# A two-layer trunk on one core: first stage in a pinned order, second shift in halves of 1024 columns, scaling on ScalarE

## The chip, the cores and the metric

The kernel runs on one core of one Trainium2 chip. The metric is the time of one execution in microseconds (us); the program is one launch. The core has five engines that work side by side, each through its own list of instructions in order: TensorE (PE; its weight loads are shown as PEld), VectorE (DVE), ScalarE (ACT), GpSimd (POOL) and SyncE (SP), which here mainly issues transfers. 16 DMA engines move data between the chip's memory and the core.

## The reference, cut to what matters

256 tokens of 2048 channels (two blocks of 128 tokens) go through two layers; everything is float32.

```python
cond = silu(c)
for l in range(2):
    sh1, sc1, g1, sh2, sc2, g2 = split(cond @ ada_w[l] + ada_b[l], 6)   # ada_w[l]: 2048 x 12288
    h = rmsnorm(x, norm_mix_g[l]) * (1 + sc1) + sh1
    y = mixer_ab(h, ...) if l == 0 else mixer_c(h, ...)
    x = x + g1 * y
    h = rmsnorm(x, norm_ffn_g[l]) * (1 + sc2) + sh2
    x = x + g2 * ((silu(h @ w1) * (h @ w3)) @ w2)                        # w1, w3: 2048 x 5632
return rmsnorm(x, final_g)
```

`mixer_ab` projects h through `w_in` (2048 x 4096) into four parts of 1024 columns, does a gated convolution over 31 tokens on two of them and a gated mixing of tokens inside chunks of 128 on the other two, and projects the result through `w_out`. `mixer_c` is a pooling over windows of tokens with a small projection.

## The kernel before, in words

**Products.** Each product of an activation with a weight is made from three of the chip's faster kind: weight and activation are split into a high part and a rest (`hi`, `lo` for weights, `ah`, `al` for activations), and hi x ah, hi x al and lo x ah are added up in PSUM. A weight block `raw` is 256 rows x 512 columns (512 KB). ScalarE casts it to `hi` (L167), VectorE subtracts (`lo`, L168), TensorE multiplies (L216, L217, L222). A `unit` is 512 rows x 512 columns: two such blocks, 24 products for the two blocks of tokens. There are 12 `raw` buffers and 4 each of `hi` and `lo`.

**Conditioning.** The six vectors of a layer are sums over the 2048 rows of `ada_w`, weighted by `cond`. They come in 512 KB blocks too, by one of two ways. On TensorE (`on_pe`, L381): products with a broadcast `cond` into the PSUM tile `ps_ada`, copied to `rows` (L395). On VectorE: multiply-adds into `accq` (512 columns, `mod_cols`, L388) or `acc` (1024 columns, `weighed` and `mod_full`, L353). Then `put_cols` turns the row into columns by small products (`ps_col`, L408) and VectorE adds the bias (L414, L417). These are Python generators: each `yield` ends a step, and the steps stand in one list, `bg`. After each unit `tick` adds the current rate to a credit and takes that many whole steps (`RATES`: 1.28 a unit in the first mixer, 0.71 in the first feed-forward).

**Entry of a stage.** An `Entry` holds what a normalised input needs. `sumsq` (ScalarE, L459) and `rstd` (VectorE and GpSimd) give the factor r of a block of tokens; `transposed` multiplies by r (VectorE, L477) and transposes 512 channels (TensorE, `tp`, L480); `prep_plain` copies that out (`xT`, ScalarE, L518). `scaled` applies scale and shift, two of four tiles on ScalarE (L500) and two on VectorE (L502), and splits the result (`ah`, ScalarE, L489; `al`, VectorE, L490). So an input can be transposed before its scale and shift are known.

**Stages that begin before their conditions are complete.** `started` takes the rows of three column blocks in four quarters of 512 rows. Ahead of a quarter it scales the input with that quarter's columns; while it multiplies, `between` advances the generators of the next quarter's scale and shift (`e.parts`), one step in each of the slots 0 to 3 and all the rest in slot 4. There are six slots in a quarter, one behind each half unit. The rate is 0 meanwhile. It is used for the first mixer (`w_in`, `params` laid out behind its first quarter) and for the first feed-forward (`w1`, `w3`). The first mixer's scale is summed on TensorE, its shift on VectorE but for the first quarter.

**Order.** The program is written as above; a planner then orders each engine's list, by the program's order as priority and by estimated durations, so that an instruction may be moved ahead of others. Transfers of blocks are issued by SP. The small parameters (`stage`, `st_b`, `prm`, `nrm`) are issued from ScalarE's queue at the start. `x` is loaded first. In the first mixer the list `bg` holds the gate (`gen_g1`, 16 steps on TensorE), the second scale (four quarters of 5 steps, on TensorE) and the second shift (four quarters of 5 steps, on VectorE, `accq`). What is left of the shift at the end is done inside the feed-forward's `started`.

Of the kernel before, what the change touches and what calls it, by code (L numbers as in the profile page):

```python
# [8 lines left out]
F32 = mybir.dt.float32  # L9
F32R = mybir.dt.float32r  # L10
AF = mybir.ActivationFunctionType
ALU = mybir.AluOpType
PSUM = bass.MemoryType.PSUM

P = 128
# [21 lines left out]
class Trunk:  # L37
# [6 lines left out]
    def __init__(self, ctx, tc, ins, out):  # L44
        self.ctx, self.tc, self.nc = ctx, tc, tc.nc
        self.i, self.out = ins, out
        self.bg = []
        self.credit = 0.0
        self.late = []
        self.fill = []  # L50

        def pool(name, bufs, **kw):
# [12 lines left out]
        self.tpp = pool("tpp", 2, space=PSUM)  # L65
        self.adap = pool("adap", 1, space=PSUM)
        self.msp = pool("msp", 1, space=PSUM)


    def consts(self):  # L70
        nc, c = self.nc, self.cpool
        i = self.i
        cs = self.wk.tile([KT, P], F32, name="cs", tag="t", bufs=3)
        nc.sync.dma_start(out=cs, in_=i["c"].rearrange("a (k p) -> (a k) p", p=P))
# [15 lines left out]

        ps = self.msp.tile([P, 512], F32, name="ps_c", tag="ms")
# [3 lines left out]
        stage = self.wk.tile([P, P], F32, name="stage", tag="t", bufs=3)  # L95
        nc.vector.memset(stage, 0.0)
# [10 lines left out]
        put("ffn_g", i["norm_ffn_g"].rearrange("l (k p) -> (l k) p", p=P), 2 * KT)  # L107
        put("conv_b", i["a_conv_b"].rearrange("l (k p) -> (l k) p", p=P), HT)
        put("a_g", i["a_norm_g"].rearrange("l (k p) -> (l k) p", p=P), HT)
        put("a_b", i["a_norm_b"].rearrange("l (k p) -> (l k) p", p=P), HT)  # L110
        put("b_bias", i["b_bias"].rearrange("l h t -> (l h) t"), HT)
        ps = self.msp.tile([P, 512], F32, name="ps_c", tag="ms")
# [5 lines left out]
        self.adab = c.tile([P, 2, 6 * KT], F32, name="adab")  # L118
        for l in range(2):
            st = self.wk.tile([P, P], F32, name="st_b", tag="t", bufs=3)  # L120
            nc.scalar.dma_start(out=st[: 6 * KT, :], in_=i["ada_b"][l].rearrange("(k p) -> k p", p=P))
            ps = self.msp.tile([P, 512], F32, name="ps_b", tag="ms")
            nc.tensor.transpose(ps[:, : 6 * KT], st[: 6 * KT, :], self.ident[: 6 * KT, : 6 * KT])
            nc.vector.tensor_copy(self.adab[:, l, :], ps[:, : 6 * KT])
# [243 lines left out]
    def mod_cols(self, l, v, q, on_pe, dst, gname=None):  # L368
# [7 lines left out]
        for u in range(4):  # L376
# [14 lines left out]
            if u < 3:  # L391
                yield
# [6 lines left out]
        yield  # L399
# [23 lines left out]
    def to_bcast(self, rows, dst, n=4):  # L423

        nc = self.nc
        hi = self.wk.tile([P, 512], F32R, name="rhi", tag="t", bufs=3)
        lo = self.wk.tile([P, 512], F32R, name="rlo", tag="t", bufs=3)
        self.split_act(rows, hi, lo)
        for j in range(n):
            ps = self.msp.tile([P, 512], F32, name="ps_bc", tag="ms")  # L430
            one = self.identr[:, 32 * j : 32 * j + 1].to_broadcast([P, P])
            nc.tensor.matmul(ps, one, hi, start=True, stop=False)
            nc.tensor.matmul(ps, one, lo, start=False, stop=True)
            nc.scalar.copy(dst[:, 512 * j : 512 * j + 512], ps)

    def norm_cols(self, e, l, sc, sh, gname):

        e.parts = [
            self.add(self.mod_cols(l, sc, q, True, e.gs, gname), self.mod_cols(l, sh, q, q == 0, e.sh))
# [33 lines left out]
    def transposed(self, b, q, r):  # L473
# [3 lines left out]
        nc.vector.tensor_scalar(xr, self.x[b][:, 512 * q : 512 * q + 512], r, None, op0=ALU.mult)  # L477
# [14 lines left out]
    def scaled(self, src, q, b, gs, sh):  # L492
# [38 lines left out]
    def between(self, gens, slot):  # L531

        for g in gens:
# [5 lines left out]
    def started(self, e, w_cols, rate, then=None):  # L539
# [8 lines left out]
        for q in range(4):  # L548
            e.act[q] = [self.scaled(e.act[q][b], q, b, e.gs, e.sh) for b in range(NB)]
            nxt = e.parts[q + 1] if q < 3 else ()  # L550
            for u, (w, col0) in enumerate(w_cols):
                self.unit(
                    w, 512 * q, col0, e.act[q], ps[u], q == 0, q == 3, lambda: self.between(nxt, 2 * u)
                )
                self.between(nxt, 2 * u + 1)
            if q == 0 and then is not None:
                then()
# [47 lines left out]
    def mixer_ab(self, e, nxt):  # L605
        nc, i = self.nc, self.i
        with ExitStack() as s:
# [14 lines left out]
            nc.scalar.dma_start(out=ws, in_=i["b_w_s"][0].rearrange("h t s -> t h s"))  # L622
            nc.scalar.dma_start(out=cwr[:CW, :], in_=i["a_conv_w"][0])
            for n, name in enumerate(("b_norm_g", "b_norm_b")):
                nc.scalar.dma_start(out=nrm[0:64:32, n, :], in_=i[name][0].rearrange("(j n) -> j n", n=512))

            def params():

# [4 lines left out]
                for hh in range(2):  # L633
                    ps = self.msp.tile([P, 4, P], F32, name="tp", tag="ms")
                    for a in range(4):
                        nc.tensor.transpose(ps[:, a, :], ws[:, 4 * hh + a, :], self.ident)
                    nc.vector.tensor_copy(wcT[:, 4 * hh : 4 * hh + 4, :], ps)
                    ps = self.msp.tile([P, 4, P], F32, name="tp", tag="ms")
                    for a in range(4):
                        k = 4 * hh + a  # L640
                        nc.tensor.transpose(ps[:, a, :CW], cwr[:CW, k * P : k * P + P], self.ident[:CW, :CW])
                    nc.vector.tensor_copy(cw[:, 4 * hh : 4 * hh + 4, :CW], ps[:, :, :CW])
                self.to_bcast(nrm[:, 0, :], bg, 2)
                self.to_bcast(nrm[:, 1, :], bb, 2)

            for b in range(NB):
                e.start(b)
                for q in range(4):
                    e.prep(b, q)
            held = self.started(e, [(w_in, 0), (w_in, DH), (w_in, 512)], RATES[0], params)  # L650
# [226 lines left out]
    def ffn(self, p, l, e, nxt, gen_g2, rest):  # L877
# [6 lines left out]
        if e.parts:  # L884
# [4 lines left out]
            ps = self.started(e, [(w1, 0), (w3, 0), (w1, 512)], RATES[1])  # L889
            held = {(1, 0): ps[0], (3, 0): ps[1], (1, 1): ps[2]}  # L890
# [76 lines left out]
    def run(self):  # L967
# [3 lines left out]
        self.x = []  # L971
        for b in range(NB):
            xb = self.xpool.tile([P, D], F32, name=f"x{b}")
            nc.sync.dma_start(out=xb, in_=i["x"][0, b * P : (b + 1) * P, :])
            self.x.append(xb)
            for q in range(4):
                self.sumsq(b, q)
# [11 lines left out]
        self.finish(mix0.parts[0][:1])  # L989
# [87 lines left out]
```

## Time and profile before

| | us |
|---|---|
| time, median of 3 runs (2012.48 to 2015.93) | 2014.81 |
| the profiled execution's own time | 2018.89 |
| span of the profiled execution | 2017.2 |
| TensorE busy in it | 1957.5 |
| granted TensorE clock, mean | 0.982 |
| moved by DMA | 540.39 MB, 268 GB/s |

The span is the time from the first to the last instruction. A group's line gives the place in the kernel, the engine, the operation, what it writes and reads, the count, then the busy time and the mean of one in ns, then the idle time of the engine in front of it and who ended it. A line of the timeline begins with its start and its duration in us; in brackets stands the idle time before it and its releaser.

### The profile page before, as it was taken

How to read it: one execution, taken by the hardware profiler on the slowest of the kernel's cores; microseconds unless marked ns; L12 is line 12 of the kernel's file. 1: busy time of each engine (PE TensorE's matmuls, PEld its weight loads, DVE VectorE, ACT ScalarE, POOL GpSimd, SP SyncE). 2: the span in 40 equal slices, each digit the busy share in tenths (PEclk: the TensorE clock that was granted, in tenths of full speed). 3: DMA queues.
4: the chain of work that ended last, by engine and by line, in shares of the span. 5: the costliest groups of instructions: out<-in, count | busy, mean ns of one | idle time of the engine just before them, and what ended most of it. 6: DMA issues, size and time to landing. Idle time of an engine off the chain costs nothing.

```text
span 2017.2 us, 24298 instructions
## 1 busy us (share of the span) xinstructions
PE 1957.5 (97%) x8896; PEld 1542.4 (76%) x8896; DVE 1420.8 (70%) x1709; ACT 840.2 (42%) x1023; POOL 34.2 (2%) x91
## 2 busy tenths in 40 slices
PE   5989999998999999999999999999999999999998
PEld 2567677777887888887878887788788888888886
DVE  2667999788778888777887788867555444554455
ACT  3234343454444334443344347544433444334443
POOL 0000000000000000000120000000000000000000
PEclk9889999989999999999999999999999999999999
DMA  9998988879888899888988887889656666566651
GB/s 329 351 369 266 339 277 284 270 252 343 294 277 327 316 341 331 300 295 316 343 308 292 289 286 264 324 276 326 198 187 191 189 189 191 183 189 190 193 184 48
DMA packets 250344, 540.39 MB, mean 268 GB/s; under 512 B 16521, under 2 KB 17849, under 8 KB 249840
## 3 DMA queue, kind: packets, MB, share of 16 engines
q1 hardware_dynamic: 248472, 536.99, 78.2%
q10 hardware_dynamic: 1752, 1.86, 0.3%
q8 instruction: 69, 1.13, 0.2%
q14 instruction: 51, 0.42, 0.1%
HBM read 536.68 MB, written 2.10 MB: 267 GB/s over the span
## 4 chain that ended last, share of the span: by engine, by line
PE 95%; DVE 2%; DMA 2%; ACT 1%; issue 0%; POOL 0%; ACTq 0%; POOLq 0%; DVEq 0%
PE mm L216 28%; PE mm L217 27%; PE mm L222 27%; PE ps_ada L381 3%; PE ps_col L408 2%; PE mt L216 1%; PE mt L217 1%; PE tp L591 1%; PE mt L222 1%; DVE accq L388 1%; PE ps_ada L315 1%; PE tp L480 1%; DMA st_b<-in_ada_b_dram 1%; PE tp L838 1%; DMA raw<-in_pool_w_dram 0%
## 5 line engine op out<-in xcount | busy, mean ns | idle before, releaser
L167 ACT CAST hi<-raw 128x1024 fp32r<-128x1024 f32 x632 | 665.1, 1053 | 986.1 <-PE mm L217 898.2
L168 DVE TENSOR_TENSOR lo<-raw,hi 128x1024 fp32r<-128x1024 f32 x632 | 771.1, 1223 | 423.6 <-ACT hi L167 413.3
L216 PE MATMUL mm<-hi,ah 128*128 128x512 f32 x1568 | 619.5, 396 | 6.0 <-ACT hi L167 3.4
L217 PE MATMUL mm<-hi,al 128*128 128x512 f32 x1568 | 613.6, 392 | 0.0
L222 PE MATMUL mm<-lo,ah 128*128 128x512 f32 x1568 | 422.9, 390 | 0.0
L216 PEld LDWEIGHTS mm<-hi,ah 128*128 128x128 f32 x1568 | 296.0, 189 | 94.3 <-ACT hi L167 14.4
L217 PEld LDWEIGHTS mm<-hi,al 128*128 128x128 f32 x1568 | 296.1, 189 | 62.9 <-DVE accq L388 1.7
L222 PEld LDWEIGHTS mm<-lo,ah 128*128 128x128 f32 x1568 | 295.6, 189 | 61.7
L216 PE MATMUL mm<-hi,hh 128*128 128x512 f32 x704 | 279.9, 398 | 0.0
L217 PE MATMUL mm<-hi,hl 128*128 128x512 f32 x704 | 277.4, 394 | 0.0
L353 DVE SCALAR_TENSOR_TENSOR acc<-raw,cond,acc 128x1024 f32<-128x1024 f32 x180 | 230.6, 1281 | 5.3 <-DMA raw<-in_ada_w_dram 3.7
L222 PE MATMUL mm<-lo,hh 128*128 128x512 f32 x704 | 194.7, 395 | 0.0
L216 PEld LDWEIGHTS mm<-hi,hh 128*128 128x128 f32 x704 | 132.1, 188 | 34.7 <-ACT hi L167 1.7
L222 PEld LDWEIGHTS mm<-lo,hh 128*128 128x128 f32 x704 | 132.1, 188 | 32.1
L217 PEld LDWEIGHTS mm<-hi,hl 128*128 128x128 f32 x704 | 132.1, 188 | 30.8
L388 DVE SCALAR_TENSOR_TENSOR accq<-raw,cond,accq 128x512 f32<-128x512 f32 x135 | 101.1, 749 | 4.8 <-DMA raw<-in_ada_w_dram 2.1
L676 DVE SCALAR_TENSOR_TENSOR co<-aT,cw,co 128x256 f32<-128x256 f32 x240 | 99.5, 479 | 0.0
L216 PE MATMUL mm<-hi,mh 128*128 128x512 f32 x160 | 64.8, 406 | 1.6 <-ACT mh L489 1.6
L599 DVE TENSOR_TENSOR gy<-mm,gate 128x512 f32<-128x512 f32 x72 | 47.1, 686 | 24.3 <-PE mm L222 23.9
L217 PE MATMUL mm<-hi,ml 128*128 128x512 f32 x160 | 63.8, 401 | 0.3 <-DVE ml L490 0.3
L381 PE MATMUL ps_ada<-raw,cond 128*32 128x512 f32 x352 | 62.3, 629 | 0.0
L600 DVE TENSOR_TENSOR x<-x,gy 128x512 f32<-128x512 f32 x72 | 47.2, 688 | 0.1
(169 smaller groups left out, 990.6 us busy)
## 6 DMA issues: line engine op xcount, KB each, us to landing
raw<-in_ffn_w_dram SPq DMA_DIRECT2D x528, 512.0 KB, 4.8
raw<-in_ada_w_dram SPq DMA_DIRECT2D x384, 512.0 KB, 5.7
raw<-in_ab_w_in_dram SPq DMA_DIRECT2D x64, 512.0 KB, 6.5
raw<-in_ab_w_out_dram SPq DMA_DIRECT2D x32, 512.0 KB, 5.7
raw<-in_pool_w_dram SPq DMA_DIRECT2D x8, 512.0 KB
x<-in_x_dram SPq DMA_DIRECT2D x2, 1024.0 KB, 6.5
gate<-in_final_g_dram SPq DMA_DIRECT2D x1, 1024.0 KB
out_dram<-x SPq DMA_DIRECT2D x2, 512.0 KB
```

Source lines behind the costliest of these rows:

```text
L167: nc.scalar.copy(hi, raw)
L168: nc.vector.tensor_tensor(lo, raw, hi.bitcast(F32), op=ALU.subtract)
L216: nc.tensor.matmul(ps[b], act[b][0][:, kk, :], hi[:, k, :], start=first and kk == 0, stop=False)
L217: nc.tensor.matmul(ps[b], act[b][1][:, kk, :], hi[:, k, :], start=False, stop=False)
L222: self.nc.tensor.matmul(ps[b], act[b][0][:, kk, :], lo[:, k, :], start=False, stop=last and kk == 3)
L353: nc.vector.scalar_tensor_tensor(acc, raw, self.cond[:, k : k + 1], acc, op0=ALU.mult, op1=ALU.add)
L381: nc.tensor.matmul(acc[32 * j : 32 * j + 32, :], self.cond[:, k : k + 1].to_broadcast([P, 32]), raws[j // 2][:, j % 2, :], start=u == 0, s ...
L388: nc.vector.scalar_tensor_tensor(acc, raws[j // 2][:, j % 2, :], self.cond[:, k : k + 1], acc, op0=ALU.mult, op1=ALU.add)
L408: nc.tensor.matmul(ps[:, a : a + 1], src[:, P * a : P * a + P], one, start=u == 0, stop=u == len(parts) - 1,)
L599: nc.vector.tensor_tensor(t, ps, g[:, 512 * q : 512 * q + 512], op=ALU.mult)
L600: nc.vector.tensor_tensor(xs, xs, t, op=ALU.add)
L676: nc.vector.scalar_tensor_tensor(co[:, k, :], src, cw[:, k, j : j + 1], co[:, k, :], op0=ALU.mult, op1=ALU.add,)
```

## The change

It has three parts.

First, the first stage gets a written order. A new method `opening` interleaves the loads of x, the first quarter of scale and shift, and the small parameters, whose transfers move from ScalarE's queue to SP. A new method `staged` replaces `started` for the first mixer: it loads and casts both blocks of a unit ahead of its products, and it puts one step of `params` (now a generator: taps, mixing weights and broadcasts of the tables) behind each half unit from the second quarter on, except in slot 4. The tables' transfers (`tables`) are issued by SP behind the first quarter. `in_order` chains all instructions of TensorE, VectorE, ScalarE and SP that are traced inside it, so that the planner can't reorder them among themselves. In the staged form `mod_cols` leaves out the step between the sum and `put_cols`.

Second, the second shift is summed by `mod_full` in two halves of 1024 columns; `started` also advances the second half during the first quarter (`more`).

Third, a flag `lean` is on from the end of the first stage to the end of the first feed-forward's `started`: the multiplication by r and all four tiles of `scaled` go to ScalarE.

```diff
+    def opening(self, e):
+        nc, c, i = self.nc, self.cpool, self.i
+        sc, sh = e.parts[0]
...
+        def tokens(b):
+            nc.sync.dma_start(out=self.x[b], in_=i["x"][0, b * P : (b + 1) * P, :])
+            for q in range(4):
+                self.sumsq(b, q)
+
+        def entry(b):
+            e.start(b)
+            for q in range(4):
+                e.prep(b, q)
...
         def put(name, ap, n):
-            nc.scalar.dma_start(out=stage[r : r + n, :], in_=ap)
+            nc.sync.dma_start(out=stage[r : r + n, :], in_=ap)
...
+        next(sc)
+        next(sc)
+        tokens(0)
+        next(sc)
         put("mix_g", ...)
+        tokens(1)
+        entry(0)
+        next(sc)
         put("ffn_g", ...)
+        ... loads of ada_b into st_b0, st_b1 ...
+        next(sh)
         put("conv_b", ...); put("a_g", ...); put("a_b", ...); put("b_bias", ...)
+        next(sh)
+        ... transposes of st_b0, st_b1 into adab ...
+        entry(1)
         ... transpose of stage into cols ...
+        self.close(sc)
+        next(sh)
+        next(sh)
+        self.close(sh)
...
-            if u < 3:
+            if u < 3 or staged:
                 yield
...
-        yield
+        if not staged:
+            yield
         self.put_cols(parts, 4, l, v, 4 * q, dst, gname)
...
-        nc.vector.tensor_scalar(xr, self.x[b][:, 512 * q : 512 * q + 512], r, None, op0=ALU.mult)
+        src = self.x[b][:, 512 * q : 512 * q + 512]
+        if self.lean:
+            nc.scalar.activation(xr, src, AF.Copy, scale=r)
+        else:
+            nc.vector.tensor_scalar(xr, src, r, None, op0=ALU.mult)
...
-            if a < 2:
+            if a < 2 or self.lean:
                 nc.scalar.activation(h[:, a, :], src[:, a, :], AF.Identity, scale=g, bias=t)
...
+    def staged(self, e, w_cols, then, extra):
+        self.rate = 0.0
...
+        for q in range(4):
+            e.act[q] = [self.scaled(e.act[q][b], q, b, e.gs, e.sh) for b in range(NB)]
+            nxt = e.parts[q + 1] if q < 3 else ()
+            for u, (w, col0) in enumerate(w_cols):
+                raws = [self.load(w, 512 * q + 256 * h, col0) for h in range(2)]
+                cuts = [self.split(raw) for raw in raws]
+                for h, (hi, lo) in enumerate(cuts):
+                    for b in range(NB):
+                        self.products(hi, lo, h, e.act[q], b, ps[u], q == 0)
+                    for b in range(NB):
+                        self.products_lo(hi, lo, h, e.act[q], b, ps[u], q == 3)
+                    self.between(nxt, 2 * u + h)
+                    if q > 0 and 2 * u + h != 4:
+                        next(extra, None)
+            if q == 0:
+                then()
...
     def started(self, e, w_cols, rate):
...
+            more = e.parts[2][1:] if q == 0 else ()
...
+            with self.in_order():
+                self.opening(e)
+                extra = params()
+                held = self.staged(e, [(w_in, 0), (w_in, DH), (w_in, 512)], tables, extra)
+                for _ in extra:
+                    pass
+            self.rate = RATES[0]
+            self.lean = True
...
-        self.finish(mix0.parts[0][:1])
...
-        shift = [self.mod_cols(0, SH2, q, False, ffn0.sh) for q in range(4)]
+        shift = [self.mod_full(0, SH2, ffn0.sh, None, (hh,)) for hh in range(2)]
         self.add(*scale, *shift)
-        ffn0.parts = list(zip(scale, shift))
+        ffn0.parts = [(scale[0], shift[0]), scale[1:2], (scale[2], shift[1]), scale[3:]]
```

More of the change, by code (lines that the diff above doesn't have):

```diff
@@ L1 @@
-from contextlib import ExitStack
+from contextlib import ExitStack, contextmanager
 import concourse.bass as bass
@@ L13 @@
 PSUM = bass.MemoryType.PSUM
+ENG = mybir.EngineType
+ORDERED = (ENG.PE, ENG.DVE, ENG.Activation, ENG.SP)
+AFTER = mybir.DependencyInfo(mybir.DependencyClass.NoSync, mybir.DependencyReason.DATA)
 P = 128
@@ L50, in __init__ @@
         self.fill = []
+        self.lean = False
         def pool(name, bufs, **kw):
@@ L111, in consts @@
         put("b_bias", i["b_bias"].rearrange("l h t -> (l h) t"), HT)
+        next(sh)
+        self.adab = c.tile([P, 2, 6 * KT], F32, name="adab")
+        for l in range(2):
+            ps = self.msp.tile([P, 512], F32, name="ps_b", tag="ms")
+            nc.tensor.transpose(ps[:, : 6 * KT], st[l][: 6 * KT, :], self.ident[: 6 * KT, : 6 * KT])
+            nc.vector.tensor_copy(self.adab[:, l, :], ps[:, : 6 * KT])
+        entry(1)
         ps = self.msp.tile([P, 512], F32, name="ps_c", tag="ms")
@@ L423, in to_bcast, with bcast_steps @@
     def to_bcast(self, rows, dst, n=4):
+        for _ in self.bcast_steps(rows, dst, n):
+            pass
+    def bcast_steps(self, rows, dst, n):
         nc = self.nc
@@ L529, in close, with between @@
             self.bg.remove(g)
-    def between(self, gens, slot):
+    def between(self, gens, slot, more=()):
+        for g in more if slot < 4 else ():
+            self.advance(g, 1)
         for g in gens:
@@ L537, in between, with in_order, started @@
                 self.close(g)
-    def started(self, e, w_cols, rate, then=None):
+    @contextmanager
+    def in_order(self):
+        traced = self.nc.cur_bb.bb.instructions
+        n = len(traced)
+        yield
+        before = {}
+        for ins in traced[n:]:
+            if ins.engine in ORDERED:
+                if ins.engine in before:
+                    self.tc.add_manual_dep(ins, before[ins.engine].name, AFTER, reason="in_order")
+                before[ins.engine] = ins
+    @contextmanager
+    def in_order(self):
+        traced = self.nc.cur_bb.bb.instructions
+        n = len(traced)
+        yield
+        before = {}
+        for ins in traced[n:]:
+            if ins.engine in ORDERED:
+                if ins.engine in before:
+                    self.tc.add_manual_dep(ins, before[ins.engine].name, AFTER, reason="in_order")
+                before[ins.engine] = ins
+    def staged(self, e, w_cols, then, extra):
+        self.rate = 0.0
+        ps = [self.banks(), self.banks()]
+        ps.append([self.tpp.tile([P, 512], F32, name=f"mt{b}", tag="tp") for b in range(NB)])
+        for q in range(4):
[14 more added lines that the diff above has]
+                then()
+        return ps
+    def started(self, e, w_cols, rate):
         self.rate = 0.0
@@ L621, in mixer_ab, with tables @@
             nc.gpsimd.memset(nrm, 0.0)
[L622 to L625, printed above, removed]
+            def tables():
+                nc.sync.dma_start(out=ws, in_=i["b_w_s"][0].rearrange("h t s -> t h s"))
+                nc.sync.dma_start(out=cwr[:CW, :], in_=i["a_conv_w"][0])
+                for n, name in enumerate(("b_norm_g", "b_norm_b")):
+                    nc.sync.dma_start(out=nrm[0:64:32, n, :], in_=i[name][0].rearrange("(j n) -> j n", n=512))
             def params():
@@ L632, in params, with taps @@
                 )
[L633 to L637, printed above, removed]
+                def taps(hh):
                     ps = self.msp.tile([P, 4, P], F32, name="tp", tag="ms")
@@ L970, in run @@
         self.consts()
[L971 to L977, printed above, removed]
+        self.x = [self.xpool.tile([P, D], F32, name=f"x{b}") for b in range(NB)]
         def cols(name):
```

57 lines of the change are left out of this document (33 added, 24 removed).

## The prediction

> **What bounds the kernel now.** I read the page first (busy shares, then the chain that ended last), then busy time by stretches, then the transfers, and only then single instructions. From the page:
>
> ```profile
> span 2017.2 us, 24298 instructions
> PE 1957.5 (97%) x8896; PEld 1542.4 (76%) x8896; DVE 1420.8 (70%) x1709; ACT 840.2 (42%) x1023; POOL 34.2 (2%) x91
> PE 95%; DVE 2%; DMA 2%; ACT 1%; issue 0%; POOL 0%; ACTq 0%; POOLq 0%; DVEq 0%
> ```
>
> TensorE bounds the whole, and the change takes no matrix product away. So it can only win where TensorE waits or runs at a low clock. The next view cuts the span at the places where that happens (columns: busy time of each engine, granted TensorE clock, share of the DMA engines, GB/s):
>
> ```profile
> core 0: us, PE busy (x) PEld busy (x) DVE busy (x) ACT busy (x) POOL busy (x), PEclk, DMA share, GB/s
> 0.00:45.89 45.89, 22.84 (x116) 8.56 (x116) 8.55 (x29) 17.10 (x38) 4.95 (x18) 0.99 0.91 323
> 45.89:140.27 94.38, 81.14 (x360) 52.48 (x361) 62.10 (x90) 25.72 (x36) 0.00 (x0) 0.86 1.00 357
> 140.27:164.10 23.83, 23.83 (x98) 19.57 (x99) 16.80 (x20) 15.78 (x20) 0.00 (x0) 0.92 0.91 333
> 427.00:442.70 15.70, 11.25 (x52) 8.73 (x50) 13.63 (x29) 9.85 (x18) 2.18 (x2) 0.73 0.79 241
> 442.70:495.60 52.90, 52.67 (x224) 42.84 (x224) 46.44 (x62) 24.90 (x32) 0.00 (x0) 0.95 0.83 291
> 495.60:509.55 13.95, 8.20 (x24) 6.36 (x23) 7.78 (x14) 4.24 (x8) 0.00 (x0) 0.63 0.87 322
> 509.55:1200.00 690.45, 690.45 (x3110) 564.01 (x3109) 544.89 (x528) 283.02 (x304) 18.41 (x61) 1.00 0.88 309
> ```
>
> The first products start at 45.89 and the first stage (three column blocks of the input projection, in four row quarters) ends at about 164.1. Up to 140 its DMA engines are full: it waits for the 64 condition blocks (scale and shift of the first mixer). The start of the first feed-forward (427 to 510) is the second hole. Behind it TensorE is full, and nothing there is changed.
>
> How full the DMA was in the first 132 us, in 40 slices of 3.3 us, and when the last condition blocks were issued:
>
> ```profile
> GB/s 51 404 376 234 362 219 167 402 387 387 387 387 383 387 387 385 376 390 387 386 387 387 387 384 387 359 178 204 322 354 374 389 387 387 362 305 311 340 308 385
> DMA packets 23749, 45.34 MB, mean 343 GB/s; under 512 B 1448, under 2 KB 2776, under 8 KB 23487
> 116.36 9.89 SPq L185 DMA_DIRECT2D raw<-in_ada_w_dram  x8
> 126.34 9.60 SPq L185 DMA_DIRECT2D raw<-in_ab_w_in_dram  x10
> ```
>
> Undisturbed the stream runs at 387 GB/s, so a block of 512 KB takes 1.355 us. It dips three times: up to 23 us, near 86 to 92 us (where the tables are laid out in one lump), and from 115 to 129 us.
>
> **The first stage, step by step.** The change moves no byte out of it. In the new order of SP the last condition block has before it 80 blocks (41.9 MB), x (2.1 MB), the tables (0.66 MB) and small vectors, 44.9 MB in all. Before, that amount is reached about 1.3 us short of 132, so the last block lands at about 130.7. After: the first slice's 51 GB/s says that the stream starts about 2.9 us in; 44.9 MB at 387 GB/s take 116.0; together 118.9. To that come two losses, bounded by what SP waited for:
>
> ```profile
> SPq L185 <- DMA raw<-in_ada_w_dram: 15.9, 23, 1.0
> SPq L185 <- DMA prm<-in_a_conv_w_dram: 7.0, 1, 7.0
> SPq L185 <- DMA stage<-in_norm_mix_g_dram: 5.9, 1, 5.9
> ```
>
> SP waits for landings of earlier transfers before it issues the next, so few are in flight. The eight small loads of the parameters and biases move from ScalarE's queue onto SP, between the blocks: there each takes a place in flight. They cost between 0 and the 5.9 us of the last row; I take 2, since big blocks stand between them. The table of the convolution's taps (31 rows) now goes through SP behind the first quarter; it costs between 0.3 us (its 124 KB at 387 GB/s) and 7.0; I take 5, nearer the row. The last block then lands at 118.9 + 2 + 5 = 126 (119 to 132): 4.7 us earlier.
>
> [...]
>
> From that landing to the end of the stage, before (timeline of TensorE, VectorE's deferred sums among it):
>
> ```profile
> 135.32 3.11 DVE L388 SCALAR_TENSOR_TENSOR accq<-raw,cond,accq 128x512 f32<-128x512 f32 x4
> 132.16 1.06 PE L381 MATMUL ps_ada<-raw,cond 128*32 128x512 f32 x8
> 133.95 1.05 PE L408 MATMUL ps_col<-pick,rows 128*128 128x1 f32 x8 [0.73 <-ACT rows L395]
> 138.57 1.84 PE L408 MATMUL ps_col<-ones,accq 128*128 128x1 f32 x8 [3.57 <-DVE accq L388]
> 147.66 0.39 PE L216 MATMUL mm<-hi,ah 128*128 128x512 f32 x1
> ```
>
> It took 164.1 - 130.7 = 33.4 us: the third block of quarter three came only after the shift's columns, part of it at half pace (7.4 us from 140.27 to 147.66), then the last quarter's three blocks, 164.1 - 147.66 = 16.4. Durations for the new order, and for the later parts, from the groups of the whole run:
>
> ```profile
> L168 DVE TENSOR_TENSOR lo<-raw,hi 128x1024 fp32r<-128x1024 f32 x632 | 771.1, 1223 | 423.6 <-ACT hi L167 413.3 <-DMA raw<-in_ada_w_dram 4.5 <-PE mm L222 2.7
> L167 ACT CAST hi<-raw 128x1024 fp32r<-128x1024 f32 x632 | 665.1, 1053 | 986.1 <-PE mm L217 898.2 <-DMA raw<-in_ada_w_dram 26.9 <-PE mt L217 20.8
> L353 DVE SCALAR_TENSOR_TENSOR acc<-raw,cond,acc 128x1024 f32<-128x1024 f32 x180 | 230.6, 1281 | 5.3 <-DMA raw<-in_ada_w_dram 3.7
> L388 DVE SCALAR_TENSOR_TENSOR accq<-raw,cond,accq 128x512 f32<-128x512 f32 x135 | 101.1, 749 | 4.8 <-DMA raw<-in_ada_w_dram 2.1 <-DVE accq L388 0.2
> L500 ACT ACTIVATE h<-xT,sh,gs 128x128 f32<-128x128 f32 x36 | 15.8, 486 | 24.2 <-DVE sh L414 24.1
> L489 ACT CAST ah<-h 128x512 fp32r<-128x512 f32 x24 | 14.7, 614 | 0.1
> L477 DVE TENSOR_SCALAR xr<-x,r 128x512 f32<-128x512 f32 x24 | 11.1, 482 | 6.2 <-PE tp L480 3.2 <-POOL r L470 3.0
> L518 ACT COPY xT<-tp 128x512 f32<-128x512 f32 x18 | 10.4, 588 | 19.5 <-PE tp L480 19.5
> L502 DVE TENSOR_SCALAR h<-xT,gs,sh 128x128 f32<-128x128 f32 x36 | 10.3, 343 | 0.1
> ```
>
> After, one half of that third block (12 products at 0.227 us, a quarter of the 16.4 / 6 per half: 2.7 us) stands ahead of the columns and the other half behind them. From the landing: the block's weights land 1.4 later and are cast (1.05): 2.4; first half 2.7: 5.1; two column groups 1.05 each: 7.2; the add 0.16, then on ScalarE for two token blocks twice (0.98 + 0.61): 10.5, beside which the second half runs; the cast of the next weights, now behind them in ScalarE's pinned order, 1.05: 11.6; last quarter 16.4: 28.0; two broadcasts of the tables in it and their copies 1: 29. A stretch at the low clock (0.63 instead of 0.39 us a product, as the 0.86 of the stage's clock says happens) adds 0 to 4; I take 1.5. So the stage ends at 126 + 30.5 = 156.5, against 164.1: **-7.6 us** (-16 to +1).
>
> What hides the rest: the earlier x, the sums of squares and the transposes stand in the 45.9 us in which the transfers run anyway. The first product itself gains little: the sixteenth block and x have landed at 2.9 + 21.7 + 5.4 + 2 = 32, then come two groups of 1.06, a copy 0.6, columns 1.05, scaling 3.2 and a cast 1.05, which is 40; the transposes of x, pinned ahead of them, may make it 43 (before: 45.89). While 12 buffers keep the stream running that costs nothing. The twelve table steps spread over quarters two to four replace the lump near 86 us. Three of them make TensorE wait for a copy queued on VectorE behind sums that wait for their blocks; a unit of two halves needs about 2 x (2.7 + 1.06 + 0.6) = 8.7 us of TensorE and the stream 10 blocks, 13.55 us, so 4.8 us a unit are free for that.
>
> **The second shift.** Sixty-four sums of 512 columns become 32 of 1024: 64 x 0.749 - 32 x 1.281 = 6.9 us less VectorE, worth nothing where TensorE is full. What counts is when the last columns come. Before, the steps are paced by 36 units of the mixer at 1.28, in whole credits 45 steps; 16 go to the gate, 20 to the scale, 9 to the shift, so that two quarters are left over for the feed-forward's start. The adds show it, quarter by quarter, and the last comes too late:
>
> ```profile
> 413.04 0.16 DVE L414 TENSOR_TENSOR sh<-ps_col,adab 128x4 f32<-128x4 f32 x1 [0.59 <-PE ps_col L408]
> 476.49 0.16 DVE L414 TENSOR_TENSOR sh<-ps_col,adab 128x4 f32<-128x4 f32 x1 [2.11 <-PE ps_col L408]
> 494.67 1.07 PE L222 MATMUL mt<-lo,ah 128*128 128x512 f32 x4
> 499.33 1.84 PE L408 MATMUL ps_col<-ones,accq 128*128 128x1 f32 x8 [3.60 <-DVE accq L388]
> 503.32 2.27 PE L216 MATMUL mm<-hi,ah 128*128 128x512 f32 x4 [2.15 <-ACT ah L489]
> 442.70:475.50 32.80, 32.57 (x132) 26.45 (x133) 27.52 (x35) 14.91 (x19) 0.00 (x0) 0.92 0.83 295
> ```
>
> From 495.60 to 509.55 only one half (2.7) and the columns (1.05) are done: 13.95 - 3.75 = 10.2 us are lost, waits and low clock together. After, a half takes eight steps: one half and one step are done at that point, seven steps remain, four taken in the first quarter and three in the second, so that no sum is left for the third boundary and the 10.2 us go. What is late next is the boundary before it, at 475.5, which now needs all columns: 14 sums of 1.281 are 17.9 us of VectorE where before 16 of 0.749 stood, 12. The row of that stretch has 27.5 of 32.8 busy; 27.5 - 12 + 17.9 - 4 x 0.343 for the scalings moved off = 32.0. VectorE just fits, and six to eight more blocks (1.355 each, up to 10.8) have to land by then, at a DMA share of 0.83. I charge 3 us of new waiting, between 0 and 10.2 (the whole stall moved forward). Net **-7.2 us**.
>
> [...]
>
> **ScalarE instead of VectorE up to the first feed-forward.** Eight normalisations and 16 scalings leave VectorE (8 x 0.482 + 16 x 0.343 = 9.3 us), and ScalarE gains as many, at about 0.6 (the copy's row) and 0.486, 12.6 us. Between 427 and 442.7 ScalarE had 9.85 of 15.70 busy, VectorE 13.63; the pace of a tile was set by both in turn. After, the tile's two ScalarE passes take 0.6 + 0.588, close to the old pace, and the first scaling 4 x 0.486 instead of 2. Between -1 and +1.5; I take 0, as neither engine becomes free.
>
> **Sum.** -7.6 - 7.2 = -14.8. The profiled execution took 2018.89, 1.7 around its span of 2017.2, and 4.1 above the median of the three runs, 2014.81. A saving in waits carries over to the median: 2014.8 - 14.8 = 2000.
>
> **Rivals.** A: the stall of the feed-forward only moves forward, from 509 to 475 (for it: the full 32.0 of 32.8; against: VectorE takes ready sums ahead of time, as it did in the 13.63 of 427 to 442.7). Then 2014.8 - 7.6 = 2007. B: the first stage stays as long, since it is bound by transfers and small loads now sit in the stream (for it: share 1.00 up to 140; against: the dips). Then 2014.8 - 7.2 = 2008. C: both, or neither works: 2011 to 2018, no change. D, the slower side: the pinned order ties TensorE to VectorE's queue, so that a quarter takes longer than its 22 blocks (29.8 us). My TensorE need of a quarter is 16.4 + 4 x 1.06 + 2.1 + 3.5 waits at the boundary = 26.3; three tied waits of 3 us and a 4 us ramp make it 39. With a first product at 43 the stage would end at 43 + 3 x 39 + 17.4 = 177, +13, and with the feed-forward's 7.2 off 2021. It decides from an average quarter of about 36.5 us on. Against it speaks that before kept 387 GB/s with TensorE at a clock of 0.86.
>
> **Chances.** A measurement here tells 0.2%, 4 us. Forecast 0.60 (alone 1990 to 2006), A 0.13, B 0.11, C 0.07, D 0.09. Faster: the first and nearly all of A and B, 0.82; same 0.09; slower 0.09. The range, 1989 to 2010, leaves C, D and the far ends out.
>
> **What would show it.** Right: last product of the first stage near 156; no dip near 86 us in the transfers; no column group waiting about 25 us before the end of the feed-forward's start, at most 3 us at its middle boundary. Wrong: column groups of the first stage waiting longer than 4 us a quarter for VectorE, a transfer rate well under 387 between the quarters, or a stall of the old size one quarter earlier.

## The result and the profile after

The changed kernel takes 2002.86 us (median of 4 runs, 2000.76 to 2004.70) beside 2015.37 before; the ratio is 0.9937, 95% interval 0.9924 to 0.9950. Forecast were 2000 and a range from 1989 to 2010. The profiled executions lie at 2018.89 and 2002.47, so the traces differ by 16.4 us where the medians differ by 12.5: the profiled execution of before lies 3.5 us above the median of its runs. All sums below are against the traces.

The page of the changed kernel, and its busy time by stretches cut at about the same places of the work (the same columns as before; the cut at 138.32 and the last three lie 9 to 39 products apart from those of before):

```profile
span 2000.7 us, 24245 instructions
PE 1949.9 (97%) x8896; PEld 1539.0 (77%) x8896; DVE 1408.7 (70%) x1650; ACT 850.9 (43%) x1047; POOL 35.5 (2%) x92
PE 92%; DMA 3%; DVE 2%; ACT 1%; issue 1%; SPq 0%; POOL 0%; POOLq 0%; DVEq 0%; ACTq 0%
```

```profile
0.00:46.15 46.15, 27.01 (x117) 11.72 (x117) 8.28 (x28) 16.89 (x37) 3.99 (x18) 0.75 0.99 362
46.15:138.32 92.17, 80.86 (x368) 53.82 (x369) 64.86 (x91) 26.70 (x36) 1.54 (x1) 0.88 0.99 351
138.32:160.40 22.08, 22.04 (x91) 17.65 (x90) 15.04 (x19) 15.78 (x21) 0.00 (x0) 0.92 0.93 328
422.00:437.97 15.97, 9.38 (x52) 7.48 (x51) 13.13 (x19) 11.22 (x23) 2.57 (x2) 0.74 0.92 315
437.97:490.00 52.03, 51.03 (x233) 42.25 (x232) 38.68 (x39) 35.63 (x58) 0.00 (x0) 0.98 0.85 291
490.00:504.00 14.00, 14.00 (x63) 11.60 (x62) 10.67 (x11) 6.25 (x7) 0.00 (x0) 1.00 0.87 293
504.00:1190.00 686.00, 686.00 (x3091) 560.25 (x3090) 541.46 (x525) 281.48 (x302) 18.39 (x61) 1.00 0.88 310
```

Transfers now show as 3% in the chain, 2% before. The granted clock of TensorE in the opening, up to the first product, is 0.75 where it was 0.99. From 490 to 504, where the old stall would be, TensorE is full at clock 1.00.

Both kernels make the same 7584 main products (`mm` and `mt`) stage by stage, so the start of the n-th one can be compared. The table says where the time went, in us; the last column counts what a stretch itself gave.

| n-th product, counted from 0 | before | after | difference | of this stretch |
|---|---|---|---|---|
| 0, first product | 45.89 | 46.15 | +0.3 | +0.3 |
| 144, third quarter begins | 117.53 | 113.05 | -4.5 | -4.7 |
| 288, first stage over | 163.98 | 160.40 | -3.6 | +0.9 |
| 1080, in the output projection | 412.87 | 408.00 | -4.9 | -1.3 |
| 1152, feed-forward begins | 442.72 | 437.97 | -4.8 | +0.1 |
| 1300, its third quarter begun | 480.09 | 476.64 | -3.4 | +1.3 |
| 1500, behind its start | 537.22 | 522.87 | -14.4 | -10.9 |
| 4000 | 1135.44 | 1121.05 | -14.4 | 0.0 |
| 4800, behind the second mixer | 1356.83 | 1340.74 | -16.1 | -1.7 |

So two thirds come from the boundary ahead of the feed-forward's last quarter, and the first stage gave about half of the 7.6 us forecast. The 1.7 us in the second layer's mixer lie in code that the change does not touch. They are the clock: the same stretch of 75 products (from the 4350th on), before and after, with the granted clock as the last figure but two:

```profile
1237.98:1265.43 27.45, 26.57 (x133) 18.00 (x131) 23.31 (x41) 17.00 (x33) 1.10 (x2) 0.94 0.67 216
1223.56:1249.44 25.88, 25.00 (x133) 17.62 (x132) 23.24 (x41) 17.06 (x33) 1.09 (x2) 1.00 0.70 218
```

The instructions are as many and the waits the same; before, TensorE ran at half clock for one stretch of 3.4 us, and the stretch took 1.6 us longer. The last section shows in which profiles that stretch is there.

The columns of the second half at the feed-forward's start, the one wait of TensorE there, the first and the last run of VectorE's sums for these columns, and the transfers of the first 132 us:

```profile
464.82 1.07 PE L256 MATMUL mm<-lo,ah 128*128 128x512 f32 x4
465.73 1.84 PE L443 MATMUL ps_col<-ones,acc 128*128 128x1 f32 x16
467.43 0.49 PE L250 MATMUL mm<-hi,ah 128*128 128x512 f32 x1
443.80 0.50 PE L250 MATMUL mm<-hi,ah 128*128 128x512 f32 x1 [1.00 <-ACT ah L536]
426.34 0.74 DVE L385 TENSOR_SCALAR acc<-raw,cond 128x1024 f32<-128x1024 f32 x1
460.94 1.28 DVE L387 SCALAR_TENSOR_TENSOR acc<-raw,cond,acc 128x1024 f32<-128x1024 f32 x1
```

```profile
GB/s 40 398 418 384 408 356 351 399 388 387 385 385 387 387 112 355 312 356 322 353 353 341 186 402 388 387 386 387 387 387 387 385 386 385 293 304 330 397 383 389
```

The column group has no wait in front of it, and from the second product behind it on they take 0.39 to 0.40 us again. VectorE began these sums ahead of time: 6 of the 16 have begun before the feed-forward's first product at 437.97, and the last ends at 462.2, 3.5 us ahead of the columns. The 1.00 us lie behind the first 12 products of the stage, not at its middle boundary.

In the first stage the dips of before up to 23 us and near 86 us are gone, but there are new ones: one slice of 112 GB/s near 46 to 49 us, and a long stretch of 312 to 356 from 49 to 72 that ends with 186. A third one stays (293 to 330 from 112 to 122 us). Three of the things that SP waited for up to 140 us, and TensorE and SP around the first product:

```profile
SPq L219 <- PE ps_ada L415: 16.2, 9, 4.6
SPq L219 <- DVE lo L202: 11.7, 2, 7.6
SPq L219 <- DMA prm<-in_a_conv_w_dram: 5.2, 1, 5.2
```

```profile
33.35 1.87 PE L443 MATMUL ps_col<-pick,rows 128*128 128x1 f32 x8 [0.38 <-DVE cols L152]
35.15 3.64 PE L415 MATMUL ps_ada<-raw,cond 128*32 128x512 f32 x16
39.58 1.87 PE L443 MATMUL ps_col<-pick,rows 128*128 128x1 f32 x8 [0.79 <-ACT rows L429]
46.15 0.79 PE L250 MATMUL mm<-hi,ah 128*128 128x512 f32 x1 [4.70 <-ACT hi L201]
38.82 0.88 SPq L219 DMA_DIRECT2D raw<-in_ab_w_in_dram  x2
47.38 9.80 SPq L219 DMA_DIRECT2D raw<-in_ada_w_dram  x8
122.40 0.37 SPq L219 DMA_DIRECT2D raw<-in_ada_w_dram  x1
```

SP issues nothing between 39.7 and 47.4: the next buffer to come free is that of the first weights, which `lo` releases (the 7.6 above), and `lo` stands in VectorE's pinned order behind the scaling. The last condition block is issued at 122.40 and lands 8.0 us later, at 130.4.

### The profile page after: what moved, and what is told of

The parts are those of the page before. It is cut to its first block, busy times and chain, and to the rows that moved or that the text cites. A ratio compares the mean times of both kernels' runs of the same rounds, so it can differ in the third digit from the quotient of the medians.

```text
span 2000.7 us, 24245 instructions
## 1 busy us (share of the span) xinstructions
PE 1949.9 (97%) x8896; PEld 1539.0 (77%) x8896; DVE 1408.7 (70%) x1650; ACT 850.9 (43%) x1047; POOL 35.5 (2%) x92
## 3 DMA queue, kind: packets, MB, share of 16 engines
q10 hardware_dynamic: 288, 1.05, 0.1%
## 4 chain that ended last, share of the span: by engine, by line
PE 92%; DMA 3%; DVE 2%; ACT 1%; issue 1%; SPq 0%; POOL 0%; POOLq 0%; DVEq 0%; ACTq 0%
PE mm L250 28%; PE mm L251 27%; PE mm L256 27%; PE ps_ada L415 2%; DMA raw<-in_ada_w_dram 1%; PE ps_col L443 1%; PE tp L691 1%; PE mt L250 1%; PE mt L256 1%; PE mt L251 1%; PE ps_ada L349 1%; PE tp L527 1%; DMA x<-in_x_dram 1%; DVE lo L202 1%; DMA raw<-in_ab_w_in_dram 1%
## 5 line engine op out<-in xcount | busy, mean ns | idle before, releaser
L387 DVE SCALAR_TENSOR_TENSOR acc<-raw,cond,acc 128x1024 f32<-128x1024 f32 x210 | 269.1, 1282 | 7.4 <-DMA raw<-in_ada_w_dram 5.7
L422 DVE SCALAR_TENSOR_TENSOR accq<-raw,cond,accq 128x512 f32<-128x512 f32 x75 | 56.3, 751 | 11.3 <-DMA raw<-in_ada_w_dram 9.6
```

The source lines that it names most:

```text
L387: nc.vector.scalar_tensor_tensor(acc, raw, self.cond[:, k : k + 1], acc, op0=ALU.mult, op1=ALU.add)
L422: nc.vector.scalar_tensor_tensor(acc, raws[j // 2][:, j % 2, :], self.cond[:, k : k + 1], acc, op0=ALU.mult, op1=ALU.add)
```

## The experiments

Times of before in the three groups of runs were 2016.5, 2016.4 and 2016.7, beside 2015.4 in the group of the changed kernel; each ratio is to before in its own group. Places and stretches are read from one profile of each kernel, by the count of products.

**One part alone.** The first two kernels separate the parts.

The halves alone, on the kernel before:

```diff
+            more = e.parts[2][1:] if q == 0 and then is None else ()
... (`between` takes `more` and advances it in the slots 0 to 3)
-        shift = [self.mod_cols(0, SH2, q, False, ffn0.sh) for q in range(4)]
+        shift = [self.mod_full(0, SH2, ffn0.sh, None, (hh,)) for hh in range(2)]
...
-        ffn0.parts = list(zip(scale, shift))
+        ffn0.parts = [(scale[0], shift[0]), scale[1:2], (scale[2], shift[1]), scale[3:]]
```

> The kernel before with the second shift in two halves of 1024 columns and nothing else: old first stage, no work moved to ScalarE. My account from the two traces: the boundary ahead of the last quarter of the feed-forward's start gave 10 us of the change, so this kernel takes about 2005 (10 less than before), its first stage ends at 164 as before, and no column group waits ahead of the last quarter. Rival (scalings on VectorE are what made the last columns late, so the move to ScalarE is needed too): the stall moves one boundary forward and stays at several us; 2009 to 2014.

Measured: 2005.53 us, ratio 0.9945 (0.9931 to 0.9960). By the count of products, 13.8 us less than before: 0.6 in the first stage, 6.1 up to the feed-forward's first product, 3.7 given back up to the 1300th, 10.9 at the last boundary. So the halves carry the gain without ScalarE's help, and the rival falls. TensorE's waits from 442 to 490 (waiter, releaser, us in total, times, longest) name most of what is given back, two waits for the scaled input, the longer one at the middle boundary:

```profile
PE mm L216 <- ACT ah L489: 2.8, 2, 1.7
```

The first stage alone, on the changed kernel:

```diff
-            more = e.parts[2][1:] if q == 0 else ()
+            more = ()
...
-            self.lean = True
...
-        shift = [self.mod_full(0, SH2, ffn0.sh, None, (hh,)) for hh in range(2)]
+        shift = [self.mod_cols(0, SH2, q, False, ffn0.sh) for q in range(4)]
...
-        ffn0.parts = [(scale[0], shift[0]), scale[1:2], (scale[2], shift[1]), scale[3:]]
+        ffn0.parts = list(zip(scale, shift))
```

> The changed kernel with the second shift again in four quarters of 512 columns and the scalings back on VectorE: the new first stage alone. My account: the first stage ends at 160.4 instead of 164.0, nothing else is gained: about 2011.5, 3.6 less than before, and the old stall of 10 us stands ahead of the last quarter of the feed-forward's start. Rival (the first stage also gives gains later, for instance through transfers that run further ahead): 2005 to 2008.

Measured: 2013.39 us, ratio 0.9986 (0.9977 to 0.9996). The stage ends at 161.0, 3.0 earlier than before, and little more follows from it up to the end (4.3 in the spans). The old stall is back in its place with its old size:

```profile
495.65 1.84 PE L443 MATMUL ps_col<-ones,accq 128*128 128x1 f32 x8 [3.60 <-DVE accq L422]
499.64 1.85 PE L250 MATMUL mm<-hi,ah 128*128 128x512 f32 x3 [2.15 <-ACT ah L536]
```

**What holds the first stage's transfers.** The table of taps in two transfers:

```diff
-                nc.sync.dma_start(out=cwr[:CW, :], in_=i["a_conv_w"][0])
+                nc.sync.dma_start(out=cwr[:16, :], in_=i["a_conv_w"][0, :16])
+                nc.sync.dma_start(out=cwr[16:CW, :], in_=i["a_conv_w"][0, 16:])
```

> The changed kernel with the table of taps (31 rows) loaded as 16 rows and 15 rows in two transfers. Theory 1: the 31 rows go through one DMA engine, which holds back every block issued behind them (the stream ran at 312 to 356 GB/s from 50 to 78 us, and SP waited 5.2 us for this table); then the wait is under 2 us, the stream is back near 387 by 70 us, and the first stage ends 3 to 5 us earlier, at about 156. Theory 2: the loss there is the table of mixing weights with its rows of 512 bytes, or SP waiting for buffers; then the stage ends within 1 us of 160.4.

Measured: 2001.22 us, ratio 0.9925 (0.9910 to 0.9940). SP's wait of 5.2 us for this table is no longer among its seven longest, which end at 2.2, and the stage ends at 158.3, 2.1 earlier, which is less than theory 1 said and more than theory 2. The first product came 1.4 us later in this execution, so between it and the stage's end 3.5 us are saved. The stream has lost the slice of 186 and the dip from 112 us on, but not the one at 46 us, and from there to 72 us it is no better than in the changed kernel, where the 31 rows run one after another from 65.67 to 72.89 us (last section):

```profile
GB/s 39 394 419 385 404 366 351 385 390 388 387 382 386 388 74 259 330 343 321 374 288 364 384 387 387 387 387 385 388 387 387 387 382 387 385 388 388 376 392 379
```

The casts ahead of the scaling (loads and splits of a quarter's first unit, too):

```diff
-            e.act[q] = [self.scaled(...) for b in range(NB)]
...
                 cuts = [self.split(raw) for raw in raws]
+                if u == 0:
+                    e.act[q] = [self.scaled(...) for b in range(NB)]
```

> The changed kernel with the loads and splits of a quarter's first unit written ahead of the scaling, so that in the pinned order of ScalarE and VectorE the casts do not wait for the scale and shift. Theory 1: SP stood still from 39.7 to 47.4 because the first weights' buffers came free only when VectorE had made lo, queued behind the scaling; now that stop goes, and the first product starts 1 to 2 us earlier; the last condition block lands about 2 us earlier and each boundary saves another 1 us: the stage ends at 156 to 158. Theory 2: the stream is held back elsewhere (tables, or the number of transfers in flight), the stop costs nothing: the stage ends within 1 us of 160.4.

Measured: 2004.26 us, ratio 0.9944 (0.9928 to 0.9961), no gain. The first product came 2.0 earlier and SP's wait for `lo` fell from 11.7 to 3.5 us, but the wait for the sums on VectorE, now behind the splits, rose from 8.7 to 14.6, and the stage ended at 159.6, 0.8 earlier. A buffer was freed earlier at the price of others: only half of theory 1 holds.

Both edits:

> The changed kernel with the table of taps in two transfers (16 and 15 rows) and the casts of a quarter's first unit ahead of the scaling. Each alone ended the first stage 2.1 and 0.8 us earlier. Theory 1 (two separate holds of one stream bound by transfers): the gains add up or more, the stage ends at 156 to 157.5, and the last condition block lands at about 126. Theory 2 (with either edit the stage is bound by something else, TensorE or VectorE at the boundaries): no earlier than 158.

Measured: 2000.86 us, ratio 0.9929 (0.9912 to 0.9946). The stage ended at 158.9 and the last block landed at 128.4: theory 2. The stream still fell, to 124 GB/s in the slice from 49.5 us on and to 263 to 351 from there up to 76 us. What holds it there lies ahead of both edits; the next two runs name it.

No chain at all (`if True:` in place of `with self.in_order():`):

> The changed kernel without the chain that pins the order of the first stage: the program is written in the same order, but the planner may move instructions ahead as before. Theory 1: the stage is bound by its transfers and their holds, not by the pinned order; the first product starts earlier or at 46, and the stage ends within 3 us of 160.4, time within 3 us of 2002.9. Theory 2: the pinning is what the first stage's gain rests on, since the planner's order put column sums and lumps of table work in the way before; without it the stage ends at 164 or later and the time is 4 or more us above 2002.9.

Measured: 2010.14 us, ratio 0.9973 (0.9963 to 0.9982); the stage ended at 167.3. Theory 2. The same program, ordered by the planner, has the first product at 39.97, six us earlier, and its last condition block lands at 129.4, 1.0 earlier, but the stage ends 6.9 later. TensorE's waits up to 165 us show the old fault, columns that wait for sums put off on VectorE. Without the chain (first two lines), and in the kernel before (third); the changed kernel has no such wait:

```profile
PE ps_col L443 <- DVE accq L422: 10.7, 3, 3.6
PE mm L250 <- ACT hi L201: 5.2, 3, 3.4
PE ps_col L408 <- DVE accq L388: 10.7, 3, 3.6
```

So pinning helps the quarters and harms the opening. The kernel with the chain around the quarters only:

```diff
-            with self.in_order():
-                self.opening(e)
+            self.opening(e)
+            with self.in_order():
```

> The changed kernel with the chain around the staged quarters only: the opening (loads, transposes, the first quarter's sums) is left to the planner. Theory 1: the pinned opening puts 16 transposes of x and a column group on TensorE ahead of the last two sums of the first shift, at the low clock, so that the first product comes at 46 and the 12 buffers are full from 39 to 47; freed, the first product comes at about 40 as in the kernel without any chain, SP does not stop there, the last condition block lands 3 to 5 us earlier (125 to 128 instead of 130.4) and the stage ends at 155 to 158. Theory 2: the early start is given back at the tables and at the boundaries, and the stage ends within 2 us of 160.4 (executions of the same opening differ by about that much).

Measured: 2001.54 us, ratio 0.9933 (0.9913 to 0.9952). The first product comes at 41.3, the dip at 46 us is gone, the last block is issued at 118.86 and lands 8.0 later, at 126.84, and the stage ends at 156.4: 3.6 and 4.0 us earlier than in the changed kernel. Theory 1. Of the 4.0 only 1.9 are left behind the feed-forward's start, and the time is 1.3 us shorter; where the rest goes was not followed. TensorE ahead of the first product, to be held against the rows of the changed kernel above:

```profile
31.02 1.05 PE L443 MATMUL ps_col<-pick,rows 128*128 128x1 f32 x8 [0.38 <-DVE cols L152]
32.01 2.78 PE L415 MATMUL ps_ada<-raw,cond 128*32 128x512 f32 x24
35.57 1.05 PE L443 MATMUL ps_col<-pick,rows 128*128 128x1 f32 x8 [0.79 <-ACT rows L429]
41.33 0.79 PE L250 MATMUL mm<-hi,ah 128*128 128x512 f32 x1 [4.70 <-ACT hi L201]
```

The first column group begins 2.3 us earlier. From there on another 2.5 come from the clock: two groups at 1.05 instead of 1.87, and 24 small products in 2.78 where 16 took 3.64 (granted clock 1.00 from 31.02 to 36.62, 0.50 from 33.35 to 41.45 in the changed kernel). This is no chance of one profile: in all seven with the pinned opening these 16 products take 3.41 to 3.64, in all four without it the 24 take 2.78. With the table in two transfers as well:

> As the kernel with the free opening, and the table of taps in two transfers of 16 and 15 rows. Theory 1 (two holds of one stream, each about 3 us): the last condition block lands at 122 to 125, the stage ends at 152 to 155, about 1996 to 1998. Theory 2 (behind the first hold TensorE or VectorE sets the pace): no more than 1 us earlier than with the free opening alone.

Measured: 1995.24 us, ratio 0.9901 (0.9882 to 0.9920). The last block is issued at 113.9 and lands at 122.0, the stage ends at 151.6. The two kernels' transfers, free opening first, then with the split table:

```profile
GB/s 52 389 414 389 404 355 348 401 389 387 384 387 387 387 386 387 387 386 337 356 333 151 405 387 387 387 387 385 387 387 387 382 388 270 334 389 391 387 387 387
```

```profile
GB/s 38 395 418 380 411 354 342 394 391 386 387 384 386 387 387 387 387 387 326 331 383 387 387 387 387 385 387 387 387 387 382 388 386 387 387 386 387 387 389 382
```

In the first there are two dips, the table's (337, 356, 333, 151) and one at 109 to 115 us (270, 334). In the second two slices are left of the first dip (326, 331), and from there on the stream is flat. The table as one transfer costs 4.9 us of landing (126.84 against 121.99) and 4.8 of the stage. By the slices about 2 of these are lost at the table itself and 1.4 in the later dip; what ties that dip to the table was not followed. The two slices that are left stand where the table of mixing weights is loaded as well; no run takes that one apart. With both holds gone the stage ends 8.8 us earlier than in the changed kernel.

**ScalarE's share.** Without the move to ScalarE:

```diff
-            self.lean = True
```

> The changed kernel with the normalisation and all scalings of the first feed-forward's start shared with VectorE again, as before the change; first stage and halves stay. Theory 1, from the run with the halves alone (its start of the feed-forward gave 13.3 us against 10.9 in the changed kernel): the move to ScalarE costs about 2.5 us, so this kernel is 2 to 3 us faster than the changed one, about 2000; its first weights' products of the feed-forward start about 5 us earlier, and the middle boundaries lose about 3 of that again. Theory 2 (the move is needed for the last columns to come in time, as predicted at no net cost): within 1 us of 2002.9 or slower.

Measured: 2004.24 us, ratio 0.9946 (0.9929 to 0.9963). By the time alone theory 2 came out. But the profiled execution's first stage ended 2.2 later although its instructions are the same (last section). From the stage's end to behind the feed-forward's start it is 0.9 us faster, 3.7 earlier at the first product, 2.8 of it given back later: theory 1's pattern with a smaller sum. With the normalisation alone back on VectorE:

```diff
-        if self.lean:
-            nc.scalar.activation(xr, src, AF.Copy, scale=r)
-        else:
-            nc.vector.tensor_scalar(xr, src, r, None, op0=ALU.mult)
+        nc.vector.tensor_scalar(xr, src, r, None, op0=ALU.mult)
```

> The changed kernel with the multiplication by r back on VectorE, the scalings left on ScalarE. Theory 1: the cost of the third part sits in the eight normalisations on ScalarE, where casts, copies and scalings stand between them and hold up the transposes; this kernel gets the early start of the feed-forward (about 5 us) and loses less than the kernel without any move at the later boundaries: 3 to 5 us faster than the changed one. Theory 2: VectorE, busy with the sums of 1024 columns, then holds up the columns at the middle boundary and gives it all back: within 1.5 us of 2002.9.

Measured: 2002.05 us, ratio 0.9936 (0.9919 to 0.9954). The time is theory 2's again. Past its first stage, which ends 1.9 later, it is 2.8 us faster up to the 1500th product (5.6 at the feed-forward's first one), not far from theory 1's 3 to 5. By these two profiles the scalings on ScalarE save a little, and the normalisations there cost more. Put together with the two edits of the first stage:

> Free opening, table of taps in two transfers, and the multiplication by r back on VectorE for the first feed-forward. In the run with that last edit alone, the feed-forward's start gave 2.8 us more than in the changed kernel. If the gains are separate, this is the fastest: 2 to 3 us under the one with the free opening and the two transfers, 1994 to 1996. If not, within 1 us of it.

Measured: 1993.23 us, ratio 0.9892 (0.9869 to 0.9916), the fastest, 2.0 below the kernel without the last edit, with overlapping intervals; in the traces the stretch from the stage's end to the 1500th product is 4.2 us shorter. It beats both kernels of the change.

## Why the prediction was right, and where a term was off

**Second shift: right in place and in cause, its charge too high.** Net 7.2 us were forecast, 10.2 gained less 3 for a new wait at the middle boundary. The stretch gave 10.9, and 1.3 were lost ahead of it, so 9.6 are left. No wait appeared at the middle boundary: the columns of the second half came without one. Of the 1.3, 0.9 is a column group of 16 products where one of 8 stood (1.84 instead of 0.95); the rest falls in the stage's first units, where the 1.00 us for the scaled input lie. VectorE did not come to the 32.0 of 32.8 us that the working had: from 437.97 to 470.40 it was busy 26.57 of 32.43. Rival A did not happen: VectorE took the sums ahead of time, as the argument against A said.

**First stage: the gain is there, the term was sized twice too large** (7.6 forecast, 3.6 in the traces, within its bounds). In the two profiles of ScalarE's share, with the same instructions in this stage, it is only 1.4 and 1.6. The tail was right: from the last landing to the end 30.5 forecast, 160.4 - 130.4 = 30.0 measured (33.4 before, with the landing estimated from the transfers). This is where pinning pays: the 10.7 us of columns waiting for VectorE are gone. The landing was wrong: 126 forecast, 130.4 measured. Of its parts the 5 us for the taps' table held in size (4.9 by the pair with the free opening). What failed is the step "While 12 buffers keep the stream running that costs nothing". The first product came at 46.15, not 40 to 43, and SP stood still for 7.6 us. With the opening free the block lands at 126.84, near the forecast, and with the table split too at 121.99, near the 118.9 + 2 that were forecast for small loads alone. Against the free opening the first product is 4.8 us late, from two sources in the pinned one: the first column group begins 2.3 us later, which the 43 allowed for, and TensorE runs at half clock from there to the scaling, another 2.5, which the working priced nowhere. So one of the signs of being wrong did show, a rate well under 387 between the quarters (312 to 356 from 49 to 72 us), and the stage's end near 156 did not come.

**The table steps, named as free, were,** as far as the runs show: TensorE waits for three of them (3.7, 1.8 and 1.2 us) in the changed kernel, and beside like waits (3.8, 1.8 and 0.4) the stream is flat in the run with the free opening and the split table. Rival D was wrong in its sign: taking the pinning away costs 7.3 us, in the run without a chain. Its ramp of 4 us in a quarter no run shows; the granted clock was 0.88 from 46.15 to 138.32 in the changed kernel. Rival B saw a true hold, a small table in the stream, but the stage did get shorter.

**ScalarE instead of VectorE: 0 forecast, about 1 lost** (0.9 by the profile without the move, inside the bounds). The working treated the two operations alike; the normalisations lose and the scalings win.

**The sum** of 14.8 stands beside 16.4 in the traces and 12.5 in the medians. That it is so near is in part luck: the first stage gave 4.0 less than forecast, the second shift 2.4 more, the mixer 1.2 for which nothing was forecast, and the 1.7 of the second layer's mixer stand where the granted clock was 0.94 before and 1.00 after, in code that is the same. The profile of before, 3.5 above its median, makes the trace's difference larger.

## What to carry to other kernels

Where a stage is bound by a full stream of transfers, count which instruction frees the buffer that the stream needs next, and place that instruction; a first product that comes late is not free once the buffers run out (here 46.15 against 41.33, and the last block landed 3.6 us later). Pin an order where the planner's guesses are bad, and leave it alone where they are good: here that was two different halves of one stage. A small transfer in a full stream may be cheaper in two: 16 + 15 rows instead of 31 saved 4.8 us of the stage here, and 2.1 with the pinned opening.

## What the runs showed of the hardware

Four profiles with the same instructions in the opening (the changed kernel, the first stage alone, and the two of ScalarE's share) have their first product at 46.15, 46.23, 48.10 and 47.83. They part at one place, here in the changed kernel and in the one without the move to ScalarE (granted clock 1.00 in the first of these rows, 0.50 in the second):

```profile
24.72 2.10 PE L415 MATMUL ps_ada<-raw,cond 128*32 128x512 f32 x16 [0.74 <-ACT rows L429]
```

```profile
25.00 3.64 PE L415 MATMUL ps_ada<-raw,cond 128*32 128x512 f32 x16 [0.73 <-ACT rows L429]
```

The same 16 small products take 2.10 or 3.64 us. It isn't the start of the burst that decides: at 25.00 us they took 1.92 in the run with the first stage alone, at 24.73 they took 3.64 in the one with the normalisation on VectorE. What decides was not shown. The parting makes 1.6 to 2.0 us at the first product (46.23 and 46.15 beside 47.83 and 48.10), and so much of a difference between two of these profiles can't be put down to their edits. That one kernel falls either way from run to run is not shown, since each has a single profile.

The second layer's mixer shows the like in the middle of the kernel. Its half-clock stretch near 1240 to 1257 us is there in four of the thirteen profiles (before, where it lasts 3.41 us from 1256.94 on, the halves alone, the first stage alone, no chain) and absent in nine. In each trace the clock changes only at multiples of 3.41 us behind its first change (19 more changes before, 21 in the changed kernel). Behind the last such mark the 4350th product starts 1.31 to 1.87 us late where the half-clock stretch is there (1.52 before), and 1.03 or 1.95 to 2.91 us where it is not (1.95 in the changed kernel). So in these profiles the 1.6 us go with where the marks fall; what places the marks was not shown.

The 31 rows of taps cost 4.9 us of the last landing against 16 and 15 rows in two transfers (126.84 and 121.99), of which only about 2 lie at the table itself. In the trace of the changed kernel the table's 31 packets of 4 KB run one after another, each beginning as the one before ends, 7.2 us in all, while 13 to 22 packets are in flight at a time; before, from 11.37 to 19.51 us, there are never two of the table's at once either. The records name no engine for a packet; one of these at a time agrees with theory 1 of the run with the table in two.

The products of the split parts, 128x512, lasted 0.39 us in the mean before (`mm<-lo,ah`), those of the conditioning, as wide and left in float32, 0.63 (`ps_ada<-raw,cond`).
